# Masked prefix sums of eight sequences, gathered at the midpoint: how the fixed first rows are loaded, and in which order listed rows go to partitions

## The chip, the cores and the metric

One core of one Trainium2 chip runs the kernel. The metric is device time in microseconds (us). Three runs of the kernel before gave 178.06, 178.50 and 179.37 us, a median of 178.5 us.

## What is computed

```
B, S, D = 8, 8192, 512            # x [B, S, D] float32, w [D, D] float32
lengths = randint(16, S, size=(B,))   # int64
mask = pos < lengths[:, None, None]
cs = cumsum(x * mask, axis=1)
mid_features = cs[arange(B), lengths // 2]
out = mid_features @ w            # [B, D]
```

The prefix sum is wanted at one place alone, so the kernel sums, for each of the 8 sequences, the rows 0 to lengths // 2 that lie below its length, and multiplies the 8 sums by w. The lengths of this draw are 1138, 5379, 511, 4113, 1809, 7542, 7716 and 1140; they are data on the chip, so the kernel learns only at run time how many rows it needs.

## The kernel before

Four rows of one sequence are one unit: 8 KB that lie together in memory. The work has three stages.

**Blind rows.** The first 256 rows (64 units) of every sequence are loaded without knowing its length. `sync` (lines 110 to 116) issues four transfers on SP's queue, each for a pair of sequences: 2 x 64 units into the 128 partitions of `xf[:, f]`, 1 MB each. Partitions 0 to 63 hold the even sequence, 64 to 127 the odd one. `s_front[f]` counts the landing.

**Listed rows.** VectorE reads the lengths and makes a list of all other units that are needed: `k_f` units for each sequence, 3161 in all for this draw. The list is cut into 25 chunks of 128, and the first chunk number (c = 0) is filled up with 39 places that fetch nothing. `rank` says which place of a chunk a partition serves: 13 times the partition's number, modulo 128. `idx` is the unit to fetch, for each partition and chunk. `gpsimd` waits for the number of chunks (`count`) and for a zeroed `xz` (`s_zero`, line 171), jumps into the middle of a long sequence of written-out code by a tree of branches (`enter`, lines 130 to 145), and issues from there one indirect transfer per chunk (line 159), from the highest chunk down to 0. Chunks 24 to 1 go into the ring `xt` of R = 8 buffers; each takes one of 8 tokens (`s_free`), which TensorE gives back when it has summed a chunk. Chunk 0 goes to `xz`. Behind the list POOL issues the two transfers of w.

**Sums and product.** TensorE waits for the four blind tiles in order, sums each by 4 matmuls (one for each row u of a unit; they stand in four column groups of the array and run side by side; weights `wf` are 0 or 1 by sequence and length), then jumps into its own sequence of code by the same tree, and sums chunk by chunk with the weights `wc`. All sums gather in `s_ps`, in four partition groups of 8. Behind chunk 0, `pe_tail` closes the four groups with 4 matmuls of 8 columns that add zero (line 312), VectorE copies `s_ps` in four quarters (`s_sb`), 4 matmuls with `fold` transpose them and add the four groups (line 318), and 16 matmuls with w (line 326) give the output, which SP and ACT store.

Of the kernel before, what the change touches and what calls it, by code (L numbers as in the profile page):

```python
# [8 lines left out]
I32 = mybir.dt.int32  # L9
ALU = mybir.AluOpType  # L10
AX = mybir.AxisListType
P = 128
# [3 lines left out]
def kernel(  # L16
# [4 lines left out]
    w: bass.AP,  # L21
    out: bass.AP,
):

# [5 lines left out]
    B, S, D = x.shape  # L32
    U = 4
# [3 lines left out]
    HEAD = 256  # L37
# [9 lines left out]
    def sb(name, shape, dt=F32):  # L47
        return ctx.enter_context(nc.sbuf_tensor(name, shape, dt))
# [4 lines left out]
    def sem(name):  # L53
        return tc.alloc_semaphore(name)

    xf = sb("xf", [P, PAIRS, U * D])
    xt = sb("xt", [P, R, U * D])
    xz = sb("xz", [P, U * D])
    wt = sb("wt", [P, KC, D])
# [8 lines left out]
    row = sb("row", [1, 4 * B])  # L68
    ones = sb("ones", [1, P])
    zero = sb("zero", [1, D])  # L70
    rank_i = sb("rank_i", [P, 1], I32)
    rank_m = sb("rank_m", [P, 1], I32)
    rank4 = sb("rank4", [P, 1])
    rank = sb("rank", [P, 1])
    q_i = sb("q_i", [P, C], I32)
# [8 lines left out]
    early = sb("early", [P, C, U, B])  # L84
    wc = sb("wc", [P, C, U, B])
    wf = sb("wf", [P, PAIRS * (U * B + 2)])
    fold_i = sb("fold_i", [P, B], I32)
    fold_m = sb("fold_m", [P, B], I32)
    fold = sb("fold", [P, B, 4])
# [8 lines left out]

    s_full = [sem(f"full{c}") for c in range(C)]
    s_front = [sem(f"front{k}") for k in range(PAIRS)]  # L100
    s_w = [sem(f"w{k}") for k in range(2)]
    s_len, s_out, s_pool, s_dve, s_pe, s_free, s_zero = (
        sem(n) for n in ("len", "out", "pool", "dve", "pe", "free", "zero"))
# [4 lines left out]


    def sync(sp):  # L110
        for f in range(PAIRS):
            sp.dma_start(out=xf[:, f],
                         in_=x[2 * f:2 * f + 2, :HEAD].rearrange("b (q u) d -> b q (u d)", u=U),
                         ).then_inc(s_front[f], 16)
        store(sp, 0)
        sp.wait_ge(s_out, 32)


    def scalar(act):
        act.dma_start(out=lens[:], in_=lens_words).then_inc(s_len, 16)  # L120
        act.memzero(xz[:]).then_inc(s_zero, 1)  # L121
        store(act, 2)

    def store(eng, j):
# [22 lines left out]


    def gpsimd(pool):
        pool.iota(rank_i[:], pattern=[[0, 1]], base=0, channel_multiplier=13)  # L150
        pool.iota(q_i[:], pattern=[[P, C]], base=0, channel_multiplier=0).then_inc(s_pool, 1)
        pool.iota(f_i[:], pattern=[[1, U]], base=0, channel_multiplier=U)
        pool.iota(fold_i[:], pattern=[[-1, B]], base=128, channel_multiplier=1)
        pool.iota(v_i[:], pattern=[[P * U, C], [1, U]], base=HEAD, channel_multiplier=0,  # L154
                  ).then_inc(s_pool, 1)
        pool.sem_inc(s_free, R)

        def gather(to, c):
            pool.indirect_dma_start(  # L159
                out=to, out_offset=None, in_=xu,  # L160
                in_offset=bass.IndirectOffsetOnAxis(ap=idx[:, c:c + 1], axis=0),
                bounds_check=B * UB - 1, oob_is_err=False,
            ).then_inc(s_full[c], 16)

        n = pool.alloc_register("n_pool")
        pool.wait_ge(s_dve, marks["count"])
        pool.load(n, count[:])
        pool.wait_ge(s_zero, 1)
        enter(pool, "gp", n)
        for c in range(C - 1, -1, -1):  # L170
            with nc.body(f"gp_c{c}", valid_engines=[pool.engine]):
                pool.wait_ge(s_dve, marks["idx"])
                if c:
                    pool.sem_inc(s_free, -1)._wait_ge(s_free, 1)  # L174
                    gather(xt[:, c % R], c)
                    pool.br(f"gp_c{c - 1}")  # L176
                else:
                    gather(xz[:], c)
                    pool.br("gp_tail")
        with nc.body("gp_tail", valid_engines=[pool.engine]):  # L180
            pool.dma_start(out=wt[:, :KC - 1],
                           in_=w[:D - P].rearrange("(p k) d -> p k d", k=KC - 1)).then_inc(s_w[0], 16)
            pool.dma_start(out=wt[:, KC - 1], in_=w[LAST]).then_inc(s_w[1], 16)
            pool.drain()
            pool.br(END)
# [5 lines left out]
    def vector(dve):  # L191
        def step(do, *args, **kw):
            if done[0]:
                dve.wait_ge(s_dve, done[0])
            do(*args, **kw).then_inc(s_dve, 1)  # L195
            done[0] += 1
# [8 lines left out]
        step(dve.memset, zero[:], 0.0)  # L205
        step(dve.memset, ones[:], 1.0)
        mark("ones")
        dve.wait_ge(s_pool, 1)
        step(ts, out=rank_m[:], in0=rank_i[:], scalar1=P - 1, scalar2=None, op0=ALU.bitwise_and)
        step(ts, out=rank[:], in0=rank_m[:], scalar1=0.0, scalar2=None, op0=ALU.add)  # L210
        step(ts, out=q[:], in0=q_i[:], scalar1=rank[:], scalar2=None, op0=ALU.add)
        step(ts, out=z[:, :, B], in0=q[:], scalar1=float(FAR), scalar2=None, op0=ALU.add)
        dve.wait_ge(s_len, 16)
# [27 lines left out]
        step(dve.tensor_reduce, out=idx[:], in_=z[:], axis=AX.X, op=ALU.add)  # L241
        mark("idx")
        step(dve.memset, wf[:], 0.0)
        dve.wait_ge(s_pool, 2)
        step(ts, out=f_m[:], in0=f_i[:], scalar1=HEAD - 1, scalar2=None, op0=ALU.bitwise_and)
        diag = wf[:].rearrange("p (f e) -> p f e", f=PAIRS)
        for h in range(2):
# [2 lines left out]
                 in0=f_m[at].unsqueeze(1).to_broadcast((64, PAIRS, U)),  # L250
                 in1=rows[at, h::2].unsqueeze(2).to_broadcast((64, PAIRS, U)), op=ALU.is_lt)
        mark("front")
        step(ts, out=rank4[:], in0=rank_m[:], scalar1=float(U), scalar2=None, op0=ALU.mult)
        step(ts, out=v4[:], in0=v_i[:], scalar1=rank4[:], scalar2=None, op0=ALU.add)
        step(tt, out=early[:].rearrange("p c u b -> p (c u) b"),
             in0=v4[:].unsqueeze(2).to_broadcast((P, C * U, B)),
# [1 line left out]
        step(tt, out=wc[:], in0=early[:], in1=ge[:].unsqueeze(2).to_broadcast((P, C, U, B)),  # L258
             op=ALU.mult)
        step(ts, out=fold_m[:], in0=fold_i[:], scalar1=31, scalar2=None, op0=ALU.bitwise_and)  # L260
        step(dve.memset, fold[:], 0.0)
        step(ts, out=fold[:, :, 0], in0=fold_m[:], scalar1=0, scalar2=None, op0=ALU.is_equal)
        mark("w")
# [11 lines left out]


    def tensor(pe):
        def add(j, weights, rows):
            return pe.matmul(s_ps[32 * j:32 * j + B], lhsT=weights, rhs=rows,  # L279
                             start=False, stop=False, skip_group_check=True,  # L280
                             tile_position=(0, 32 * j))

        n = pe.alloc_register("n_pe")
        pe.wait_ge(s_dve, marks["ones"])
        for to, width in ((s_ps, D), (o_ps, P)):
            for j in range(4):
                pe.matmul(to[32 * j:32 * j + 32, :width], lhsT=zero[:, :32], rhs=zero[:, :width],  # L287
                          start=True, stop=False, skip_group_check=True, tile_position=(0, 32 * j))
        pe.wait_ge(s_dve, marks["row"])
        pe.matmul(bc_ps[:, :4 * B], lhsT=ones[:], rhs=row[:], start=True, stop=True,  # L290
                  ).then_inc(s_pe, 1)
        pe.load(n, count[:])
        pe.wait_ge(s_dve, marks["front"])
        for f in range(PAIRS):
            pe.wait_ge(s_front[f], 16)
            for u in range(U):
                at = (f * U + u) * B
                add(u, wf[:, at:at + B], xf[:, f, u * D:(u + 1) * D])
        pe.wait_ge(s_dve, marks["w"])
        enter(pe, "pe", n)  # L300
        for c in range(C - 1, -1, -1):
            with nc.body(f"pe_c{c}", valid_engines=[pe.engine]):
                pe.wait_ge(s_full[c], 16)
                rows = xt[:, c % R] if c else xz[:]
                for u in range(U):
                    mm = add(u, wc[:, c, u], rows[:, u * D:(u + 1) * D])
                if c:
                    mm.then_inc(s_free, 1)
                pe.br(f"pe_c{c - 1}" if c else "pe_tail")
        with nc.body("pe_tail", valid_engines=[pe.engine]):  # L310
            for j in range(4):
                mm = pe.matmul(s_ps[32 * j:32 * j + 32, :8], lhsT=zero[:, :32], rhs=zero[:, :8],  # L312
                               start=False, stop=False, skip_group_check=True,
                               tile_position=(0, 32 * j))
            mm.then_inc(s_pe, 1)
            for k in range(KC):
                pe.wait_ge(s_dve, marks["s"] - KC + k + 1)
                pe.matmul(mf_ps[k][:, :4 * B], lhsT=s_sb[:, k * P:(k + 1) * P],  # L318
                          rhs=fold[:].rearrange("p b r -> p (b r)"),
                          start=True, stop=True).then_inc(s_pe, 1)  # L320
            for k in range(KC):
                pe.wait_ge(s_dve, marks["mf"] - KC + k + 1)
                if k in (0, KC - 1):
                    pe.wait_ge(s_w[k // (KC - 1)], 16)
                for j in range(4):
                    mm = pe.matmul(o_ps[32 * j:32 * j + 32, :P], lhsT=mf_sb[:, k],  # L326
                                   rhs=wt[:, k, j * P:(j + 1) * P], start=False,
                                   stop=(k == KC - 1), skip_group_check=True,
                                   tile_position=(0, 32 * j))
            mm.then_inc(s_pe, 1)  # L330
            pe.br(END)
# [41 lines left out]
```

## Time and profile before

| | us |
|---|---|
| median of the three runs | 178.5 |
| the profiled execution | 178.0 |
| its span, first to last instruction | 175.9 |
| PE busy | 48.7 |
| POOL busy | 28.3 |
| DVE busy | 13.7 |

The profiled execution took 178.0 us, of which 175.9 us are the span and 2.1 us lie around it. No compute engine is busy for 30% of the span. The transfers move 31.25 MB: 4.20 MB on SP's queue (the blind rows and half of the output) and 26.95 MB on POOL's (the listed rows, 25.9 MB, and w, 1.05 MB). "DMA share" is the mean busy share of the 16 DMA engines in a stretch, "GB/s" what they moved.

### The profile page before, as it was taken

Reading aid. Unit: us, or ns where it says so; the run is one execution under the profiler, and the core shown is the slowest. Engines: PE = TensorE matmul, PEld = TensorE weight load, DVE = VectorE, ACT = ScalarE, POOL = GpSimd, SP = SyncE. Lnnn points to the kernel's source line nnn. Section 1 sums busy time; section 2 is a strip of 40 time slices with the busy share of each in tenths; the row PEclk is TensorE's granted clock in tenths of the full one; section 3 lists DMA queues with packets and bytes.
Section 4 is the critical chain, followed back from the end, with each engine's and each line's share of the span. In section 5 each row is a group of like instructions: output and inputs, shape, how many; then the busy total and the mean of one; then the engine's idle time right before and its main releaser. Section 6 shows DMA issues by size and latency. Waiting matters only on the chain. (4 is left out here: it accounts for less than half of the span.)

```text
span 175.9 us, 843 instructions
## 1 busy us (share of the span) xinstructions
PE 48.7 (28%) x298; PEld 7.4 (4%) x298; DVE 13.7 (8%) x41; ACT 3.2 (2%) x2; POOL 28.3 (16%) x36
## 2 busy tenths in 40 slices
PE   5100000004000000400040000439728756677590
PEld 1100000000000000000000000002100000000040
DVE  5793000000000000000000000000000000000040
ACT  6000000000000000000000000000000000000000
POOL 3078400000000000000000000005774445200000
PEclk9999999999999999999999999999985585856798
DMA  0159999951111111111111110003999999999800
GB/s 17 56 181 345 335 306 313 311 168 50 56 52 52 54 52 54 52 54 52 54 54 52 54 52 39 4 7 86 360 421 438 421 417 417 429 425 419 366 29 4
DMA packets 4389, 31.25 MB, mean 178 GB/s; under 512 B 485, under 2 KB 517, under 8 KB 709
## 3 DMA queue, kind: packets, MB, share of 16 engines
q0 software_dynamic: 3824, 26.95, 40.6%
q1 hardware_dynamic: 538, 4.20, 5.9%
q8 instruction: 5, 0.08, 0.2%
q14 instruction: 2, 0.02, 0.0%
q10 hardware_dynamic: 20, 0.01, 0.0%
HBM read 31.46 MB, written 0.02 MB: 179 GB/s over the span
## 5 line engine op out<-in xcount | busy, mean ns | idle before, releaser
L159 POOL DMA_INDIRECT xt<-in_x_dram,idx x24 | 24.7, 1031 | 120.9 <-POOLq L174 110.0
L279 PE MATMUL s_ps<-xt,wc 128*8 128x512 f32 x192 | 33.9, 820 | 20.5 <-DMA xt<-in_x_dram,idx 15.3
L279 PE MATMUL s_ps<-xf,wf 128*8 128x512 f32 x32 | 7.6, 1041 | 98.4 <-DMA xf<-in_x_dram 98.4
L195 DVE COPY s_sb<-s_ps 128x128 f32<-128x128 f32 x4 | 1.2, 291 | 154.1 <-PE s_ps L312 154.0
L279 PEld LDWEIGHTS s_ps<-xt,wc 128*8 128x8 f32 x192 | 3.7, 92 | 50.8 <-DMA xt<-in_x_dram,idx 38.0
L279 PEld LDWEIGHTS s_ps<-xf,wf 128*8 128x8 f32 x32 | 0.5, 91 | 103.9 <-DMA xf<-in_x_dram 70.2
L287 PE MATMUL s_ps<-zero 1*32 1x512 f32 x8 | 1.9, 1055 | 1.9 <-DVE ones L195 1.9
L195 DVE TENSOR_TENSOR wc<-early,ge 128x1952 f32<-128x1952 f32 x1 | 2.2, 2243 | 0.0
L195 DVE TENSOR_TENSOR early<-v,bc_ps 128x1952 f32<-128x1952 f32 x1 | 2.2, 2186 | 0.0
L121 ACT ACTIVATE xz<-xz 128x2048 uint32<-128x2048 uint32 x1 | 1.9, 1909 | 0.0
L279 PE MATMUL s_ps<-xz,wc 128*8 128x512 f32 x8 | 1.5, 832 | 0.6 <-DMA xz<-in_x_dram,idx 0.6
L318 PE MATMUL mf_ps<-fold,s_sb 128*128 128x32 f32 x8 | 1.4, 286 | 0.4 <-DVE s_sb L195 0.4
L121 ACT ACT_TABLE_LOAD x1 | 1.3, 1283 | 1.5 <-SPq L45 1.5
L326 PE MATMUL o_ps<-wt,mf_sb 128*32 128x128 f32 x32 | 1.3, 285 | 0.0
L318 PEld LDWEIGHTS mf_ps<-fold,s_sb 128*128 128x128 f32 x8 | 1.2, 188 | 0.6 <-DVE s_sb L195 0.5
L159 POOL DMA_INDIRECT xz<-in_x_dram,idx x1 | 1.0, 987 | 0.3 <-issue 0.3
L290 PE MATMUL bc_ps<-row,ones 1*128 1x32 f32 x2 | 0.6, 406 | 1.0 <-DVE row L195 1.0
L154 POOL IOTA v_i<- 128x244 int32 x1 | 0.8, 819 | 0.0
L195 DVE COPY mf_sb<-mf_ps 128x32 f32<-128x32 f32 x4 | 0.8, 192 | 0.4
L195 DVE TENSOR_REDUCE idx<-z 128x61 int32<-128x549 f32 x1 | 0.7, 726 | 0.0
L195 DVE TENSOR_TENSOR ge<-q,bc_ps 128x488 f32<-128x488 f32 x1 | 0.7, 662 | 0.7 <-PE bc_ps L290 0.7
L195 DVE TENSOR_TENSOR z<-ge,bc_ps 128x488 f32<-128x488 f32 x1 | 0.7, 661 | 0.0
(43 smaller groups left out, 10.3 us busy)
## 6 DMA issues: line engine op xcount, KB each, us to landing
xf<-in_x_dram SPq DMA_DIRECT2D x4, 1024.0 KB
wt<-in_w_dram POOLq DMA_DIRECT2D x1, 768.0 KB, 19.6
xt<-in_x_dram,idx POOLq DMA_INDIRECT x24, 17.5
wt<-in_w_dram POOLq DMA_DIRECT2D x1, 256.0 KB, 19.6
lens<-in_lengths_dram ACTq DMA_DIRECT2D x1, 0.1 KB
xz<-in_x_dram,idx POOLq DMA_INDIRECT x1, 18.7
out_dram<-o_sb SPq DMA_DIRECT2D x1, 8.0 KB
out_dram<-o_sb ACTq DMA_DIRECT2D x1, 8.0 KB
```

The source lines that it names most:

```text
L121: act.memzero(xz[:]).then_inc(s_zero, 1)
L154: pool.iota(v_i[:], pattern=[[P * U, C], [1, U]], base=HEAD, channel_multiplier=0,).then_inc(s_pool, 1)
L159: pool.indirect_dma_start(out=to, out_offset=None, in_=xu, in_offset=bass.IndirectOffsetOnAxis(ap=idx[:, c:c + 1], axis=0), bounds_check=B ...
L195: do(*args, **kw).then_inc(s_dve, 1)
L279: return pe.matmul(s_ps[32 * j:32 * j + B], lhsT=weights, rhs=rows, start=False, stop=False, skip_group_check=True, tile_position=(0, 32 * j))
L287: pe.matmul(to[32 * j:32 * j + 32, :width], lhsT=zero[:, :32], rhs=zero[:, :width], start=True, stop=False, skip_group_check=True, tile_po ...
L290: pe.matmul(bc_ps[:, :4 * B], lhsT=ones[:], rhs=row[:], start=True, stop=True,).then_inc(s_pe, 1)
L318: pe.matmul(mf_ps[k][:, :4 * B], lhsT=s_sb[:, k * P:(k + 1) * P], rhs=fold[:].rearrange("p b r -> p (b r)"), start=True, stop=True).then_i ...
L326: mm = pe.matmul(o_ps[32 * j:32 * j + 32, :P], lhsT=mf_sb[:, k], rhs=wt[:, k, j * P:(j + 1) * P], start=False, stop=(k == KC - 1), skip_gr ...
```

## The change

Three things change. The blind rows come as eight transfers, one per sequence, of 64 units each into 64 partitions; of the last sequence only rows 128 to 255 come this way (32 units), and ACT zeroes the 32 partitions that stay empty. The places of a chunk are dealt to partitions by another formula (four `iota` of 32 partitions and a multiply-add on VectorE in place of the factor 13). The 128 rows left out are fetched last, behind chunk 0 and ahead of w, one row per partition (`xb`), and summed in `pe_tail` by 4 matmuls of 128 columns, one for each quarter of the columns; these take the place of the four closing matmuls.

```diff
     def sync(sp):
-        for f in range(PAIRS):
-            sp.dma_start(out=xf[:, f],
-                         in_=x[2 * f:2 * f + 2, :HEAD].rearrange("b (q u) d -> b q (u d)", u=U),
-                         ).then_inc(s_front[f], 16)
+        for b in range(B):
+            skip = P if b == B - 1 else 0
+            at = 64 * (b % 2)
+            sp.dma_start(out=xf[at + skip // U:at + HU, b // 2],
+                         in_=x[b, skip:HEAD].rearrange("(q u) d -> q (u d)", u=U),
+                         ).then_inc(s_front[b // 2], 16)
...
     def scalar(act):
         act.dma_start(out=lens[:], in_=lens_words).then_inc(s_len, 16)
-        act.memzero(xz[:]).then_inc(s_zero, 1)
+        act.memzero(xz[:])
+        act.memzero(xf[64:64 + P // U, PAIRS - 1]).then_inc(s_zero, 1)
...
     def gpsimd(pool):
-        pool.iota(rank_i[:], pattern=[[0, 1]], base=0, channel_multiplier=13)
+        for k in range(4):
+            pool.iota(base[32 * k:32 * k + 32], pattern=[[0, 1]],
+                      base=64 * (k % 2) + 8 * (k // 2) + 63 * 8 * k,
+                      channel_multiplier=16).then_inc(s_pool, 1)
+        pool.wait_ge(s_pool, 4)
+        pool.iota(p_i[:], pattern=[[0, 1]], base=0, channel_multiplier=1)
         pool.iota(q_i[:], pattern=[[P, C]], base=0, channel_multiplier=0).then_inc(s_pool, 1)
...
         with nc.body("gp_tail", valid_engines=[pool.engine]):
+            pool.dma_start(out=xb[:], in_=x[B - 1, :P]).then_inc(s_back, 16)
             pool.dma_start(out=wt[:, :KC - 1],
...
-        dve.wait_ge(s_pool, 1)
-        step(ts, out=rank_m[:], in0=rank_i[:], scalar1=P - 1, scalar2=None, op0=ALU.bitwise_and)
-        step(ts, out=rank[:], in0=rank_m[:], scalar1=0.0, scalar2=None, op0=ALU.add)
+        dve.wait_ge(s_pool, 5)
+        step(ts, out=p4[:], in0=p_i[:], scalar1=2, scalar2=None, op0=ALU.logical_shift_right)
+        step(stt, out=rank[:], in0=p4[:], scalar=-63.0, in1=base[:], op0=ALU.mult, op1=ALU.add)
...
         step(dve.memset, wf[:], 0.0)
-        dve.wait_ge(s_pool, 2)
+        step(dve.memset, wb[:], 0.0)
+        dve.wait_ge(s_pool, 6)
...
+        step(tt, out=wb[:, B - 1:], in0=p_i[:], in1=rows[:, B - 1:], op=ALU.is_lt)
...
         for f in range(PAIRS):
-            pe.wait_ge(s_front[f], 16)
+            pe.wait_ge(s_front[f], 32)
+            if f == PAIRS - 1:
+                pe.wait_ge(s_zero, 1)
...
         with nc.body("pe_tail", valid_engines=[pe.engine]):
+            pe.wait_ge(s_back, 16)
             for j in range(4):
-                mm = pe.matmul(s_ps[32 * j:32 * j + 32, :8], lhsT=zero[:, :32], rhs=zero[:, :8],
-                               start=False, stop=False, skip_group_check=True,
-                               tile_position=(0, 32 * j))
+                mm = add(j, wb[:], xb[:, j * P:(j + 1) * P], slice(j * P, (j + 1) * P))
             mm.then_inc(s_pe, 1)
```

With the new formula the places e, e + 16, e + 32 and so on of a chunk fall to partitions 4m to 4m + 3 and 32 partitions further, where m = e for e below 8; for e = 8 to 15 they fall to the upper 64 partitions in the same way.

What SP issues at the start, before (`xf` are the blind rows; the sizes are those of the tile that is written):

```order
4 L112 DMA xf<-in_x_dram 128x1x2048 x4
5 L126 DMA out_dram<-o_sb 2x8x128
6 L341 UNCONDITIONAL_BRANCH
7 L45 NO_OP
8 L368 UNCONDITIONAL_BRANCH
```

And now:

```order
4 L120 DMA xf<-in_x_dram 64x2048 x7
5 L120 DMA xf<-in_x_dram 32x2048
6 L135 DMA out_dram<-o_sb 2x8x128
7 L359 UNCONDITIONAL_BRANCH
8 L47 NO_OP
```

Four transfers of 128 partitions became seven of 64 and one of 32. On ACT, before:

```order
2 L120 DMA lens<-in_lengths_dram 1x16
3 L121 ACT_TABLE_LOAD
4 L121 ACTIVATE xz<-xz 128x2048
5 L126 DMA out_dram<-o_sb 2x8x128
6 L341 UNCONDITIONAL_BRANCH
```

And now, with the second zeroing, behind which POOL's and TensorE's waits for `s_zero` now stand:

```order
2 L128 DMA lens<-in_lengths_dram 1x16
3 L129 ACT_TABLE_LOAD
4 L129 ACTIVATE xz<-xz 128x2048
5 L130 ACTIVATE xf<-xf 32x2048
6 L135 DMA out_dram<-o_sb 2x8x128
```

The end of the list on PE, before (`xz` is chunk 0, `s_ps` the sums):

```order
156 L135 COMPARE_AND_BRANCH
157 L279 MATMUL s_ps<-xz,wc 8x512 x4
158 L309 UNCONDITIONAL_BRANCH
159 L312 MATMUL s_ps<-zero 32x8 x4
160 L318 MATMUL mf_ps<-fold,s_sb 128x32 x4
161 L326 MATMUL o_ps<-wt,mf_sb 32x128 x16
```

And now, with the matmuls on the 128 rows that come last:

```order
156 L144 COMPARE_AND_BRANCH
157 L296 MATMUL s_ps<-xz,wc 8x512 x4
158 L328 UNCONDITIONAL_BRANCH
159 L296 MATMUL s_ps<-xb,wb 8x128 x4
160 L336 MATMUL mf_ps<-fold,s_sb 128x32 x4
161 L344 MATMUL o_ps<-wt,mf_sb 32x128 x16
```

The four matmuls of row 159 changed in place; nothing else moved on PE.

## Rows read from the trace of the kernel before

**Rows 1.** The page: 40 equal slices of the span (4.4 us each).
```profile
DMA  0159999951111111111111110003999999999800
GB/s 17 56 181 345 335 306 313 311 168 50 56 52 52 54 52 54 52 54 52 54 54 52 54 52 39 4 7 86 360 421 438 421 417 417 429 425 419 366 29 4
```

**Rows 2.** The longest waits of the whole span: waiting, waited for, total us, times, longest.
```profile
POOL xt L159 <- POOLq L174: 110.0, 10, 99.8
PE s_ps L279 <- DMA xf<-in_x_dram: 98.4, 4, 33.5
PE s_ps L279 <- issue: 5.2, 1, 5.2
```

**Rows 3.** Timeline of the head: SP's four issues and the first alone, ACT, DVE, POOL.
```profile
0.97 65.96 SPq L112 DMA_DIRECT2D xf<-in_x_dram  x4
...
0.97 0.68 SPq L112 DMA_DIRECT2D xf<-in_x_dram  x1
...
2.76 1.91 ACT L121 ACTIVATE xz<-xz 128x2048 uint32<-128x2048 uint32 x1
...
3.72 0.14 DVE L195 TENSOR_SCALAR count<-up_i 1x1 int32<-1x1 int32 x1
...
9.08 1.19 POOL L159 DMA_INDIRECT xt<-in_x_dram,idx  x1 [6.78 <-DVE wf L195]
...
19.16 0.99 POOL L159 DMA_INDIRECT xt<-in_x_dram,idx  x1 [0.30 <-issue]
```

**Rows 4.** Timeline of PE: first and last of four blind tiles, then chunks; start us, us.
```profile
39.46 1.90 PE L279 MATMUL s_ps<-xf,wf 128*8 128x512 f32 x8 [33.55 <-DMA xf<-in_x_dram]
...
110.03 1.90 PE L279 MATMUL s_ps<-xf,wf 128*8 128x512 f32 x8 [17.79 <-DMA xf<-in_x_dram]
...
117.15 9.39 PE L279 MATMUL s_ps<-xt,wc 128*8 128x512 f32 x72 [5.23 <-issue]
```

**Rows 5.** Two longer stages, in the same columns.
```profile
64.00:108.00 44.00, 3.79 (x16) 0.24 (x16) 0.00 (x0) 0.00 (x0) 0.00 (x0) 1.00 0.13 53
128.00:165.00 37.00, 23.13 (x116) 1.80 (x120) 0.00 (x0) 0.00 (x0) 11.90 (x13) 0.67 1.01 422
```

**Rows 6.** Timeline of PE's weight loads, chunk 1 and chunk 0 as they land.
```profile
164.47 0.12 PEld L279 LDWEIGHTS s_ps<-xt,wc 128*8 128x8 f32 x8 [2.38 <-DMA xt<-in_x_dram,idx]
166.96 0.12 PEld L279 LDWEIGHTS s_ps<-xz,wc 128*8 128x8 f32 x8 [2.37 <-DMA xz<-in_x_dram,idx]
```

**Rows 7.** The page's DMA queues, POOL's and SP's: packets, MB, share of 16 engines.
```profile
q0 software_dynamic: 3824, 26.95, 40.6%
q1 hardware_dynamic: 538, 4.20, 5.9%
```

**Rows 8.** Stages: from:to, length, busy us per engine, PEclk, DMA share, GB/s.
```profile
0.00:5.00 5.00, 2.35 (x16) 0.58 (x16) 3.13 (x17) 3.19 (x2) 1.43 (x9) 1.00 0.07 21
...
20.00:25.00 5.00, 0.00 (x0) 0.00 (x0) 0.00 (x0) 0.00 (x0) 0.15 (x1) 1.00 1.04 318
...
30.00:35.00 5.00, 0.00 (x0) 0.00 (x0) 0.00 (x0) 0.00 (x0) 0.00 (x0) 1.00 1.02 313
...
125.00:130.00 5.00, 2.34 (x24) 0.23 (x16) 0.00 (x0) 0.00 (x0) 3.79 (x4) 1.00 0.97 387
```

**Rows 9.** The chain that ended last, in order of time: start us, us, what.
```profile
148.22 18.70 DMA xz<-in_x_dram,idx
...
166.97 1.47 PE s_ps L279 x8
168.44 0.22 PE s_ps L312 x8
...
170.41 1.24 PE o_ps L326 x32
```

**Rows 10.** The later transfer of w: its issue in the timeline, then issue to landing.
```profile
149.77 0.60 POOL L183 DMA_DIRECT2D wt<-in_w_dram  x1
...
wt<-in_w_dram POOLq DMA_DIRECT2D x1, 256.0 KB, 19.6
```

More of the change, by code (lines that the diff above doesn't have):

```diff
@@ L56 @@
     xf = sb("xf", [P, PAIRS, U * D])
+    xb = sb("xb", [P, D])
     xt = sb("xt", [P, R, U * D])
@@ L70 @@
     zero = sb("zero", [1, D])
-    rank_i = sb("rank_i", [P, 1], I32)
-    rank_m = sb("rank_m", [P, 1], I32)
+    p_i = sb("p_i", [P, 1], I32)
+    p4 = sb("p4", [P, 1], I32)
+    base = sb("base", [P, 1], I32)
     rank4 = sb("rank4", [P, 1])
@@ L86 @@
     wf = sb("wf", [P, PAIRS * (U * B + 2)])
+    wb = sb("wb", [P, B])
     fold_i = sb("fold_i", [P, B], I32)
@@ L100 @@
     s_front = [sem(f"front{k}") for k in range(PAIRS)]
+    s_back = sem("back")
     s_w = [sem(f"w{k}") for k in range(2)]
@@ L252, in vector @@
         mark("front")
-        step(ts, out=rank4[:], in0=rank_m[:], scalar1=float(U), scalar2=None, op0=ALU.mult)
+        step(ts, out=rank4[:], in0=rank[:], scalar1=float(U), scalar2=None, op0=ALU.mult)
         step(ts, out=v4[:], in0=v_i[:], scalar1=rank4[:], scalar2=None, op0=ALU.add)
@@ L277, in tensor, with add @@
     def tensor(pe):
-        def add(j, weights, rows):
-            return pe.matmul(s_ps[32 * j:32 * j + B], lhsT=weights, rhs=rows,
+        def add(j, weights, rows, cols=slice(0, D)):
+            return pe.matmul(s_ps[32 * j:32 * j + B, cols], lhsT=weights, rhs=rows,
                              start=False, stop=False, skip_group_check=True,
```

## The prediction, made before the changed kernel ran

> **What bounds the kernel now.** I read the slices of the page first. The DMA engines are full twice, for some 20 us near the start and 40 us before the end; between them lie about 80 us in which they move 50 GB/s and then almost nothing [rows 1]. The list of waits says who stands there: POOL waits 99.8 us at a stretch for a token to issue its next gather, and TensorE waits 98.4 us for the blind rows [rows 2]. These are one wait: POOL has issued 8 gathers by 20.2 us [rows 3], the ring is full, and tokens come back only when TensorE has summed a chunk, which in its program stands behind the four blind tiles. The first of them is summed at 39.5 us, the fourth at 110.0, and the first chunk at 117.2 [rows 4].
>
> So the blind rows bound the first 110 us. When they are alone they move at 53 GB/s with a DMA share of 0.13, which is 2 of 16 engines, 26.5 GB/s each [rows 5]. Two is also the number of sequences in one transfer. With all 16 busy on gathers the rate is 422 GB/s, again 26.4 for each [rows 5], and a chunk of 1.05 MB lands every 2.49 us [rows 6]. After 117 us the kernel is bound by these transfers alone: TensorE's burst took 9.39 us for 9 chunks, 1.04 each at the 2.4 GHz level [rows 4]; even the slowest group of four in these rows, 1.90, is under 2.49.
>
> **The change part by part.** One transfer per sequence hands 64 units, not 2 sequences, as its outermost dimension. I take it that these are dealt over 16 engines, 4 units each. The 4.19 MB of blind rows then need no longer 110 us. TensorE's wait of 98.4 us goes, and with it POOL's. What is late next is the volume itself: 26.95 MB on POOL's queue and 4.20 on SP's [rows 7], over 16 engines. The sum follows the bytes.
>
> *Start.* In the first 5 us of before, 21 GB/s, 0.105 MB, were moved [rows 8]; at 53 GB/s these take 2.0 us, so data flows from 3.0 us. SP was held for 65.96 us by its four issues, of which the first alone took 0.68 [rows 3]; the later ones waited behind two engines with 64 units of each transfer. With 4 units per engine I expect eight issues like the first, 5.5 us, ahead of the data they start.
>
> *Gathers start later.* POOL waits for `s_zero` before it enters its code. Before, the zeroing ended at 2.76 + 1.91 = 4.67, `count` stood at 3.86 and the first gather was issued at 9.08 [rows 3], 4.4 behind the zeroing. Now a second zeroing of the same width, 1.9 us, lies ahead of that signal: 6.6 us, first gather at 11.0, first data some 2 us later, at 13.1 (before, the slices show the engines filling about 2 us behind 9.08 [rows 1]). Behind the waiting POOL stand all gathers. Until then blind rows fill the engines, so the delay is covered unless these are through before 13.1. POOL's four extra iotas and VectorE's three extra instructions (0.14 for the one shown [rows 3]) are below 1 us and lie inside the same cover.
>
> *Rate of the blind rows.* No row shows blind rows on 16 engines. The top is 422 GB/s. The nearest row with blind and gathered rows in flight together is 20 to 35 us: engines full (share 1.00 to 1.04), yet only 313 to 318 GB/s [rows 8]. I take 313. The bottom is half of 422, 211 GB/s, reached if writing into 64 of the 128 partitions gives half of the paths.
>
> The Trainium skill states just that: "SBUF — State Buffer", section "Door 1: The DMA port swizzle (why `[64,N]` ≈ `[32,N]`)", says that partitions 0 to 63 reach only 8 of 16 ports and measured 196 GB/s there against 328 for 128 partitions. By it the sum would stand at the bottom; this case's trace has no transfer of that shape on 16 engines to show it. Its page "DMA: Bandwidth & Descriptors", section "Back-pressure in remote DMA", says that stalled writes hold up an engine's other queues too; the 313 to 318 GB/s at full share [rows 8] fit this, but do not prove it.
>
> *Sum.* Blind rows by SP's queue: 8 x 0.524 - 0.262 = 3.93 MB. From 3.0 to 13.1 at 313 GB/s 3.16 MB are through. The other 0.77 MB share the engines evenly with 0.77 MB of gathers: 1.54 / 0.313 = 4.9 us, to 18.0. TensorE then sums the last blind tile (1.9) and enters its chunk code (5.2 [rows 2]), about 25 us. By then the 8 issued gathers have 8.39 - 0.77 = 7.6 MB left at 18.0, 18 us of work, so tokens come back in time and the engines never run dry; that cover is gone only if the blind rows land after about 30 us. The gathers are POOL's 26.95 MB less 1.05 of w, 25.90. Remaining: 25.90 - 0.77 = 25.13 MB at 422: 59.5, to 77.5. A settling loss as at 125 to 130 us (387 in place of 422 for 5 us [rows 8]): 0.4. Chunk 0 lands at 77.9.
>
> *Even dealing.* Chunk 0 moves 89 units of 128, but landed 2.49 us behind the chunk before it, as a full one does [rows 6]: some engine had 8. By the new formula none has more than 6, some 1.86 us. This 0.6 us is in the sum already, as I counted bytes.
>
> *The end.* Before, chunk 0 landed at 148.22 + 18.70 = 166.92 and the span ended at 175.9: 8.95 us, of which 1.47 + 0.22 are its sums and the closing matmuls [rows 9]. Now 0.26 MB of `xb` land 0.62 behind chunk 0, which its 1.47 us of matmuls hide. The closing becomes 4 matmuls of 128 columns; 16 of those took 1.24 [rows 9], so 4 take 0.31, and waiting and starting them apart I allow 0.25 more than before: 9.2 in all. Bounds: 0 if the overlap is as good as before, 1 if xb lands late. w lies 0.62 later: its later part landed at 149.77 + 19.6 = 169.4 [rows 10], and the matmuls on w run from 170.41 [rows 9]; a slack of 1.0 becomes some 0.6 (0.62 later, used 0.25 later), so nothing. Without that slack each 0.1 us would cost 0.1.
>
> So the span is 77.9 + 9.2 = 87.1, with 2.1 around it 89.2. The median of the runs lies 0.5 above the profiled execution; I forecast 89.7 us.
>
> **The rivals.** *Full rate.* The blind rows run at 422: done at 3.0 + 9.3 = 12.3, before the gathers' data at 13.1. Then 13.1 + 25.90 / 0.422 = 74.5, and with 0.4, 9.2, 2.1 and 0.5 it is 86.7. For it: two engines alone reach their full 26.5 each [rows 5]; against it: the 313 at full share.
>
> *Half rate.* At 211 GB/s 2.13 MB are through at 13.1. For the other 1.80 MB and as much of gathers, three of four packets would go to one half: 2/3 of 422, 281 GB/s, 12.8 us, to 25.9. Then 24.1 / 0.422 = 57.1: 83.0, and 95.2 in all. The port rule quoted above is this rival.
>
> *Slow gathers.* The 313 to 318 GB/s may not be the mixture but the first 8 chunks themselves, the units of the last sequences. Then 8.39 MB take 26.8 in place of 19.9: 6.9 more, on top of the full rate 93.6, on top of the forecast up to 96.6. For it: 14 of the 16 engines had no blind rows then, and yet the whole was a quarter slower. Against it: the later chunks, also consecutive units, ran at 422.
>
> *It doesn't do what it says, and is slower.* If one transfer of one sequence, which is one unbroken piece of memory, went to a single engine, the blind rows would take 3.93 MB / 26.5 GB/s = 148 us, to 151. From the last blind tile on, before needed 178.0 - 110.0 = 68.0 us: 219 us, plus nothing hidden. It decides once the blind rows move below 3.93 MB / 107 us = 37 GB/s. For it: two sequences went with two engines. Against it: the program's rows show 64 x 2048 with 64 outermost.
>
> **How the numbers follow.** Forecast (between 88 and 92): 0.40. Half rate: 0.27. Full rate: 0.17. Slow gathers: 0.11. A gather rate that stays at 313 throughout (25.1 / 0.313 = 80 in place of 59.5, about 110 us): 0.03. One engine: 0.02. The range goes from 85.0, a little under full rate, to 97.5, above half rate and slow gathers. A change of 1% is about what can be told from none here. Faster by over 1%: 0.98; within: 0.00; slower: 0.02.
>
> **What would show it.** Right: SP's eight issues over by 10 us; blind tiles summed before 25 us; POOL's first gather at about 11; no slice of the DMA below 7 tenths between 4 and 78 us; chunks landing every 2.49 us once the blind rows are in; VectorE's copy of `s_ps` about 2 us after chunk 0. Wrong: blind rows at 211 or 422 GB/s in the stage from 5 to 13 us name a rival at once; stages above 25 us at 313 name slow gathers; tokens that POOL waits for while the DMA share falls mean that TensorE's entry has become the bound; a first blind tile after 30 us means few engines.

## The result and the profile after

| | before | after |
|---|---|---|
| median of the runs, us | 178.28 | 95.96 |
| ratio to before, 95% interval | 1 | 0.5377 (0.5349 to 0.5405) |
| profiled execution, us | 178.0 | 95.83 |
| its span, us | 175.9 | 93.7 |
| blind rows on the move, GB/s | 53 | 215 to 226 |
| gathers alone, GB/s | 422 | 421 |

Some executions of these kernels take 0.8 to 3.5 us longer than the rest, most of them at a lower granted clock; the medians leave them out, but the traces of two experiments ("The dealing of before" and "The first part alone") are of such executions. The time fell by 82.3 us, nearly to half. The range given, 85.0 to 97.5 us, holds the time; the forecast itself, 89.7 us, is 6.3 us too low, and the half-rate rival's 95.2 is 0.8 off. What happened is that rival, not the rate that the forecast chose.

The slices of the changed kernel's page answer to [rows 1]; a slice is now 2.3 us:

```profile
DMA  0999999999999999999999999999999999995000
GB/s 0 238 224 224 220 224 213 224 224 399 413 420 430 406 423 413 420 416 430 413 427 416 430 427 413 430 402 427 416 430 416 427 413 430 408 410 227 9 10 4
```

The engines are full from the second slice almost to the end; the long empty stretch is gone. But eight slices, from 2.3 to 21.1 us, move only 213 to 238 GB/s at full share. The engines are busy there and carry half of what they carry later.

The stages of the changed kernel, in the columns of [rows 8]:

```profile
5.00:10.00 5.00, 0.86 (x6) 0.62 (x10) 3.66 (x14) 1.59 (x1) 0.00 (x0) 1.00 1.00 215
10.00:15.00 5.00, 3.55 (x16) 0.12 (x8) 4.86 (x5) 0.00 (x0) 0.00 (x0) 1.00 1.00 215
15.00:20.00 5.00, 1.76 (x10) 0.12 (x8) 0.39 (x3) 0.00 (x0) 3.38 (x4) 1.00 1.05 226
...
25.00:30.00 5.00, 0.00 (x0) 0.00 (x0) 0.00 (x0) 0.00 (x0) 0.99 (x1) 1.00 1.01 415
30.00:35.00 5.00, 0.54 (x4) 0.13 (x8) 0.00 (x0) 0.00 (x0) 0.00 (x0) 1.00 1.01 418
...
26.00:70.00 44.00, 23.11 (x144) 2.94 (x144) 0.00 (x0) 0.00 (x0) 18.54 (x20) 0.87 1.01 421
```

215 GB/s from 5 to 15 us is 0.51 of the 421 that the gathers reach (last row). The two rows from 25 to 35 us are of the same first chunks that ran at 313 to 318 in the kernel before [rows 8]: here they run at full rate, with no blind rows in flight.

The timeline of the changed kernel: SP's issues, ACT's zeroings, POOL's first gather, the last blind tile and the first chunks. It answers to [rows 3, 4].

```profile
0.97 5.04 SPq L120 DMA_DIRECT2D xf<-in_x_dram  x8
...
2.76 1.91 ACT L129 ACTIVATE xz<-xz 128x2048 uint32<-128x2048 uint32 x1
...
4.68 1.91 ACT L130 ACTIVATE xf<-xf 32x2048 uint32<-32x2048 uint32 x1
...
15.71 1.19 POOL L173 DMA_INDIRECT xt<-in_x_dram,idx  x1 [12.62 <-POOLq L188]
...
22.04 1.90 PE L296 MATMUL s_ps<-xf,wf 128*8 128x512 f32 x8 [1.90 <-DMA xf<-in_x_dram]
...
34.46 8.04 PE L296 MATMUL s_ps<-xt,wc 128*8 128x512 f32 x56 [10.52 <-issue]
```

SP is free after 6.0 us, the last blind tile is summed at 22.0 in place of 110.0. Two things are later than foreseen: the first gather, issued 9.1 us behind the second zeroing's end at 6.59, and TensorE's entry into its chunk code, 10.5 us in place of 5.2. A third thing is seen only in the packet records of the trace: the first gather, issued at 15.7, moves its first packet at 20.0 us, and the last packet of the blind rows ends at 21.0. Blind rows and gathers hardly ran beside each other.

The chain that ended last, answering to [rows 9]:

```profile
64.71 17.86 DMA xt<-in_x_dram,idx
82.57 0.04 issue
82.61 3.93 PE s_ps L296 x24
86.54 0.02 issue
86.56 0.30 DVE s_sb L210
```

The last transfer in the chain is chunk 1, not chunk 0: from 82.61 on TensorE works without a pause on chunk 1, chunk 0 and xb (8 records each).

### The profile page after: what moved, and what is told of

The parts are those of the page before. It is cut to its first block, busy times and chain, and to the rows that moved or that the text cites. A ratio compares the mean times of both kernels' runs of the same rounds, so it can differ in the third digit from the quotient of the medians.

```text
span 93.7 us, 856 instructions
## 1 busy us (share of the span) xinstructions
PE 48.6 (52%) x298; PEld 7.4 (8%) x298; DVE 14.2 (15%) x43; ACT 5.1 (5%) x3; POOL 28.7 (31%) x41
## 5 line engine op out<-in xcount | busy, mean ns | idle before, releaser
L173 POOL DMA_INDIRECT xt<-in_x_dram,idx x24 | 24.0, 1001 | 38.6 <-POOLq L188 34.4
L130 ACT ACTIVATE xf<-xf 32x2048 uint32<-32x2048 uint32 x1 | 1.9, 1905 | 0.0
L160 POOL IOTA base<- 32x1 int32 x4 | 0.5, 124 | 0.8 <-SPq L47 0.6
## 6 DMA issues: line engine op xcount, KB each, us to landing
xz<-in_x_dram,idx POOLq DMA_INDIRECT x1, 18.4
```

What stands on the lines that cost most here:

```text
L130: act.memzero(xf[64:64 + P // U, PAIRS - 1]).then_inc(s_zero, 1)
L160: pool.iota(base[32 * k:32 * k + 32], pattern=[[0, 1]], base=64 * (k % 2) + 8 * (k // 2) + 63 * 8 * k, channel_multiplier=16).then_inc(s_p ...
L173: pool.indirect_dma_start(out=to, out_offset=None, in_=xu, in_offset=bass.IndirectOffsetOnAxis(ap=idx[:, c:c + 1], axis=0), bounds_check=B ...
```

## The experiments

Two theories stood against each other after the result. *Halves*: a transfer into 64 partitions of one half reaches half of the ways into the chip's memory, so blind rows run at half rate. *Queue*: SP's queue, or transfers of 0.5 MB, give 215 GB/s wherever they write. The code fences are excerpts: `...` and the remarks behind `#` are added, and lines that only follow from an edit are left out.

**Blind rows over all partitions.** Two rows a partition in place of four; zeroing, weights and matmuls follow.

```diff
-            at = 64 * (b % 2)
-            sp.dma_start(out=xf[at + skip // U:at + HU, b // 2],
-                         in_=x[b, skip:HEAD].rearrange("(q u) d -> q (u d)", u=U),
+            sp.dma_start(out=xf[skip // V:, b],          # V = 2
+                         in_=x[b, skip:HEAD].rearrange("(q v) d -> q (v d)", v=V),
...
```

> The changed kernel, but every sequence's 64 blind units are laid out as 128 half units of 2 rows over all 128 partitions (the last sequence's 128 rows over the upper 64). Halves theory (a transfer into 64 partitions of one half reaches half of the paths, so the blind rows ran at 215 GB/s): the blind rows move at about 415 GB/s from 3 us on and are in by 13 us; the first gather, issued at 15.7 in the changed kernel, limits what is left, so 90 to 93.5 us. Queue theory (SP's queue, or transfers of 0.5 MB, give 215 GB/s wherever they write): blind rows at 215 GB/s until 20 us, 96 us as before.

Measured: 89.91 us, ratio 0.5068 (0.5044 to 0.5093), 6.0 us faster than the changed kernel and just below the expected span. Its stages, in the same columns:

```profile
5.00:10.00 5.00, 1.28 (x6) 0.62 (x10) 3.70 (x13) 0.64 (x1) 0.00 (x0) 1.00 1.02 411
10.00:15.00 5.00, 4.53 (x32) 0.69 (x24) 4.79 (x6) 0.00 (x0) 3.10 (x2) 1.00 0.78 247
15.00:20.00 5.00, 0.10 (x4) 0.00 (x0) 0.18 (x1) 0.00 (x0) 3.78 (x5) 0.92 0.97 377
```

From the same queue, with the same 0.5 MB each, the blind rows move at 411 GB/s. The queue theory falls. From 10 to 15 us the engines are no longer full: now the gathers' start is bare.

**An earlier start of the gathers.** The zeroing signal is split, so that POOL waits for the first zeroing alone.

```diff
-        act.memzero(xz[:])
+        act.memzero(xz[:]).then_inc(s_zero, 1)
         act.memzero(xf[64:64 + P // U, PAIRS - 1]).then_inc(s_zero, 1)
...
-                pe.wait_ge(s_zero, 1)
+                pe.wait_ge(s_zero, 2)
```

> The changed kernel with the zeroing signal split, so that POOL waits for the first zeroing alone and TensorE for both. The first gather moves from 15.7 to between 10 and 14 us, so that gathers run beside blind rows. Halves theory: blind rows alone use half of the paths, mixed with gathers two thirds (281 GB/s), so some 6 us of mixing gain 0.9 us: 95.1 us, at most 1.5 faster. Queue theory: the gathers find the other half of every engine free and mix at 420 GB/s: 3 us faster, 93 us. If the gathers' start does not matter at all: 96.0.

Measured: 95.05 us, ratio 0.5365 (0.5335 to 0.5394): 0.9 us faster, though the two intervals overlap. That is the size that halves give, but not for their reason. A stage of this kernel, in the same columns, and two pieces of the chain that ended last:

```profile
15.00:20.00 5.00, 2.12 (x12) 0.12 (x8) 0.65 (x3) 0.00 (x0) 3.80 (x4) 1.00 1.03 224
...
65.69 18.44 DMA xz<-in_x_dram,idx
...
84.17 1.31 PE s_ps L296 x16
```

The first gather is issued at 14.14 in place of 15.71 (so the delay is not the zeroing alone), yet the rate stays at half, 224 GB/s and not 281 or 420. In the packet records the first gather's data move from 19.9 us, where they moved from 20.0 in the changed kernel. The mixing for which both theories gave a price did not take place, and this run does not decide between them. Of the 1.0 us by which the profiled execution is shorter, 0.3 lie ahead of chunk 0's landing (84.13 against 84.4 us). The sums of chunk 0 and xb make up most of the rest: 1.31 us at a granted clock of 1.00, where the changed kernel, at 0.50 from 84 to 86 us, needed 2.0.

**Both edits.** The two diffs above together.

> Both edits: blind rows over 128 partitions and the split zeroing signal. Halves theory: blind rows in by 12.5, first gather issued at about 11, data from 13, engines full almost throughout: 87 to 90 us. Queue theory: as with the split signal alone, 93 us.

Measured: 89.60 us, ratio 0.5038 (0.5004 to 0.5072). Within what halves gave; the split signal adds 0.3, which the intervals do not tell from nothing. The first gather is issued at 10.94 in place of 11.60.

**The disputed cost by itself.** A program of loads alone, stage by stage, executed once. Of its lines the fence shows the transfers; loops and waits are left out.

```diff
+            sp.dma_start(out=xf[:64, b], in_=rows(b, 0, 256))        # 0 to 63, 8 times
+            sp.dma_start(out=xf[32:96, b], in_=rows(b, 256, 256))    # 32 to 95, 8 times
+            sp.dma_start(out=xf[:, b, :2 * D], in_=rows(b, 512, 256, 2))
+            sp.dma_start(out=xf[:64, b], in_=rows(b, 768, 256))      # even b, and beside it
+            act.dma_start(out=xf[64:, b], in_=rows(b, 768, 256))     # odd b
+            pool.dma_start(out=xt[:, k], in_=rows(6, 512 * k, 512))  # alone, 8 times
+            act.dma_start(out=xf[:, 0], in_=pair(0, 1024, 256))      # beside 8 more of pool's
+            act.dma_start(out=xf[:8, k], in_=pair(0, 1280 + 16 * k, 16))  # the same
```

> Leaves out the whole computation: it only moves rows of x into the chip, in stages one behind the other, and stores zeros. Stages, with the halves theory's rates: 8 transfers of 64 units into partitions 0 to 63: 215 GB/s; the same into partitions 32 to 95: about 415; the same rows as half units into all 128: about 415; even sequences into 0 to 63 on SP's queue beside odd ones into 64 to 127 on ACT's: 215 to 415; 8 plain loads of 128 units on POOL's queue alone: 420; the same beside one transfer of 2 x 64 units on two engines: 300 to 320, as at 20 to 35 us of the kernel before; the same beside two-engine transfers that write only the 4 partitions which these engines serve anyway: about 420. Queue theory: 215 in each stage on SP's queue. If memory, not the way into the chip, made the mixture slow, the last stage is at 300 to 320 too.

A stretch inside each stage, in their order (from:to, length, DVE, POOL, PEclk, DMA share, GB/s):

```profile
5.00:22.00 17.00, 0.00 (x0) 0.00 (x0) 1.00 1.01 206
32.00:36.00 4.00, 0.00 (x0) 0.00 (x0) 1.00 0.99 418
46.00:49.00 3.00, 0.00 (x0) 0.00 (x0) 1.00 1.00 408
54.00:68.00 14.00, 0.00 (x0) 0.00 (x0) 1.00 1.01 232
78.00:92.00 14.00, 0.00 (x0) 0.00 (x0) 1.00 1.01 425
102.00:118.00 16.00, 0.00 (x0) 0.00 (x0) 1.00 1.02 308
...
150.00:162.00 12.00, 0.00 (x0) 0.00 (x0) 1.00 1.01 427
```

Row 1 against row 2: same queue, sizes and number of partitions; 0 to 63 gives 206 GB/s, 32 to 95 gives 418 once settled (311 from 26 to 30 us, in the first transfers). So what counts is that both halves are written, not how many partitions. Row 3 is the end of its stage; from 38 to 44 us the same transfers ran at 317 to 358, for which no run here has a cause. Row 6 rebuilds the mixture of the kernel before: loads of 128 partitions that run at 425 alone fall to 308, all queues together, when a transfer of two engines (53 GB/s alone, from 128 to 140 us) writes across all partitions. In row 7 two engines again carry another queue's transfers, but write only partitions 0 to 7: 427. The rows are read in much the same way, so the writing is the likely cause of the slow mixture. The two stages differ in one thing more, transfers of 64 KB in place of one of 1 MB, and no row shows which engine writes which partitions.

**The dealing of before.**

```diff
-        for k in range(4):
-            pool.iota(base[32 * k:32 * k + 32], pattern=[[0, 1]],
...
+        pool.iota(rank_i[:], pattern=[[0, 1]], base=0, channel_multiplier=13)
...
```

> The changed kernel with the dealing of before (places 13 times the partition, modulo 128). The prediction's even dealing was worth 0.6 us: chunk 0's slowest engine has 8 units in place of 6. So chunk 0 comes 2.5 us behind chunk 1, not 1.9: 96.6 us. Rival: chunk 1's matmuls at the low clock, 1.9 us, already cover what the dealing saves, or other engines lag by more: 96.0, no difference.

Measured: 95.97 us, ratio 0.5367 (0.5318 to 0.5416). No difference can be told, but the interval reaches 0.9 us to either side, so the 0.6 is not excluded either. The weight loads of chunk 1 and chunk 0 in the timeline of this kernel:

```profile
82.61 0.12 PEld L292 LDWEIGHTS s_ps<-xt,wc 128*8 128x8 f32 x8 [2.37 <-DMA xt<-in_x_dram,idx]
84.99 0.12 PEld L292 LDWEIGHTS s_ps<-xz,wc 128*8 128x8 f32 x8 [2.26 <-DMA xz<-in_x_dram,idx]
```

And the same two of the changed kernel:

```profile
82.61 0.12 PEld L296 LDWEIGHTS s_ps<-xt,wc 128*8 128x8 f32 x8 [2.37 <-DMA xt<-in_x_dram,idx]
84.50 0.12 PEld L296 LDWEIGHTS s_ps<-xz,wc 128*8 128x8 f32 x8 [1.76 <-DMA xz<-in_x_dram,idx]
```

Even dealing does bring chunk 0 earlier, 1.89 in place of 2.38 us behind chunk 1. In the changed kernel it could not be summed sooner than that: TensorE takes 1.90 for chunk 1 in this stretch (granted clock 0.65 from 82 to 84 us, 0.50 from 84 to 86, the 1.2 GHz level), and chunk 0 lands at 84.4, just before it is free. So some 0.5 us are gained up to the start of chunk 0; whether they reach the total is not shown.

**Without the third part.** All 256 rows of the last sequence come blind, the closing matmuls of before are back.

```diff
-            skip = P if b == B - 1 else 0
+            skip = 0
...
-            pool.dma_start(out=xb[:], in_=x[B - 1, :P]).then_inc(s_back, 16)
...
-                mm = add(j, wb[:], xb[:, j * P:(j + 1) * P], slice(j * P, (j + 1) * P))
+                mm = pe.matmul(s_ps[32 * j:32 * j + 32, :8], lhsT=zero[:, :32], rhs=zero[:, :8],
...
```

> The changed kernel without its third part: all 256 rows of the last sequence come blind, the closing matmuls of before are back, and no second zeroing is needed. Halves theory: 0.26 MB more at 215 GB/s before the list, 1.2 us; POOL starts 1.9 us earlier, worth 0.6 as with the split signal; the end without xb 0.2 us shorter: 96.3 to 96.5. Rival: xb covers the sums of chunk 0, as it seems meant to, and its loss costs over 1 us more: 97.5.

Measured: 96.14 us, ratio 0.5399 (0.5359 to 0.5439). Against the changed kernel no difference can be told; against the one with the split signal, whose POOL starts about as early (14.14 against 14.50 us here), xb seems to be worth 1.1 us, about the 1.2 of its bytes at half rate, though these intervals overlap too. In the traces chunk 0 lands at 85.86 us here and at 84.13 there.

**The first part alone.** Both of the last two edits: the kernel before with eight transfers.

> The kernel before with the first part of the change alone: eight transfers of one sequence each. If the first part carries the whole gain, 96.5 to 97.2 us (the two other parts are worth 0.3 to 1.2 together). If the three parts work only together, over 99.

Measured: 97.61 us, ratio 0.5461 (0.5425 to 0.5498), 0.4 above the expected span. So the first part brings 80.7 of the 82.3 us, the other two together some 1.7. Without xb the dealing seems to be worth 1.5 (97.61 against 96.14, though the intervals of their ratios still overlap a little). The weight loads of chunk 0 come 1.88 us behind those of chunk 1 with it and 2.49 without it, which would explain 0.6 of that.

**A faster version: 384 blind rows over all partitions.** The gap of 10 to 20 us is to be filled with rows that would otherwise be listed.

```diff
-    HEAD = 256
+    HEAD = 384                                          # V = 3; skip = 0, no xb
...
```

> An attempt at a faster kernel: 384 blind rows of each sequence, 3 to a partition over all 128 partitions, no xb, no second zeroing. Blind rows: 6.29 MB, in by about 18 us, so that the engines stay full until the gathers have started (with 256 rows spread they moved only 292 and 370 GB/s between 10 and 20 us, about 2.4 us lost). 23 chunks in place of 25; some 0.5 MB are read in vain. Halves theory with that gap filled: 87.5 to 88.7 us, against 89.6 with 256 rows. If the wider blind stage only delays POOL's code by as much: 89.6 to 90.5.

Measured: 90.89 us, ratio 0.5096 (0.5045 to 0.5147), a miss. The gap is filled (419 GB/s from 10 to 15 us), but a new one opens where none was expected (two stages of this kernel, same columns):

```profile
25.00:35.00 10.00, 0.96 (x4) 0.00 (x0) 0.00 (x0) 0.00 (x0) 0.00 (x0) 0.67 1.01 419
37.00:41.00 4.00, 4.00 (x24) 0.70 (x20) 0.00 (x0) 0.00 (x0) 1.98 (x2) 0.60 0.55 180
```

The 8 gathers issued early are through at 37 us, and POOL got its next token only at 37.9.

**The same with 11 buffers.**

```diff
-    R = 8
+    R = 11
```

> The kernel with 384 blind rows and a ring of 11 buffers in place of 8. With 8, the engines ran dry between 37 and 41 us (98 to 348 GB/s), since TensorE's entry into its chunk code ended only at 35.1 us and tokens came late. If that is the loss, 3 buffers more (7.5 us of transfers) cover it: no stage below 0.95 from 5 to 75 us, 2.5 us faster, 88.0 to 88.7 us. If the dip only moves (TensorE enters its code later still while the engines are full), 90.5 to 91.2.

Measured: 87.71 us, ratio 0.4944 (0.4907 to 0.4981), 0.3 below the expected span, 8 us under the changed kernel and the fastest seen. The same stretch, in the same columns:

```profile
37.00:41.00 4.00, 4.00 (x28) 0.74 (x24) 0.00 (x0) 0.00 (x0) 1.98 (x2) 0.59 1.02 420
```

## Why the prediction was right, and where it was off

- *That the blind rows bound the first 110 us, and the volume what follows*: right. SP's issues ended at 6.0, the last blind tile came before 25 us, no slice fell below 9 tenths until the list was in, chunks landed every 2.49 us. The first part alone shows it: 97.61 us.
- *16 engines for 64 units*: right. The share is 1.00 where 2 sequences outermost gave 0.13. The rival of one engine, 219 us, falls.
- *Rate of the blind rows*: this step failed. "I take 313", from the stage of before in which blind and gathered rows were mixed; it was 215, and the prediction's own sign for this rival, about 211 GB/s in the stage from 5 to 13 us, came true. The row of 313 was not a measurement of 16 engines on blind rows but of gathers beside a transfer of two engines, and the probe gives both: 308 for the mixture, 206 for 64 partitions of one half. The bottom of the bound, half of 422, was the value to take. By that rule, in the Trainium skill's "SBUF — State Buffer", section "Door 1: The DMA port swizzle (why `[64,N]` ≈ `[32,N]`)", the rate follows from the ports that the partitions reach; the trace agrees, 206 GB/s for partitions 0 to 63 and 418 for 32 to 95.
- *Half rate, as rival*: right in the rate and within 0.8 us. It let gathers run beside the blind rows at 281 GB/s from 13.1 us and these end at 25.9. That mixing did not happen: the first gather was issued at 15.7 and moved data from 20.0, the rate stays at half up to 21.1 us and is 399 GB/s in the next slice. For the sum it makes no difference: with the gathers only behind the blind rows, 3.0 + 3.93 / 0.211 + 25.90 / 0.422 is 83.0 as well. So the rival's time holds, and its rate for the mixture, two thirds, stays untested.
- *Slow gathers*: fell. The same eight chunks run at 415 to 418 GB/s when no blind rows are in flight.
- *Gathers start at 11.0*: wrong, 15.7. The prediction took 4.4 us from the zeroing to the first gather, as before; it was 9.1. As foreseen, blind rows covered it: with the split signal the first gather is issued 1.6 us earlier and its data move 0.1 earlier. (VectorE has two instructions more, 43 against 41, not three; nothing hangs on it.)
- *TensorE enters its code in 5.2*: wrong, 10.5. The cover held with 8 buffers in the changed kernel; with wider blind rows it did not, and cost 3.2 us (90.89 against 87.71).
- *Even dealing, 0.6*: right for chunk 0 (1.89 us behind chunk 1, 2.38 without it); its effect on the total is too small for these runs.
- *The end, 9.2 us behind chunk 0*: right. Chunk 0 landed at 84.4 (issued at 66.0, 18.4 us to landing) and the span ended at 93.7, 9.3 us.

The size that was missed is in the main one term, the rate of the blind rows. With 215 GB/s, and the gathers behind them, the prediction's sum ends the list at 3.0 + 18.3 + 61.4 = 82.7 us in place of 77.5: 5.2 of the 6.3. Chunk 0 then landed 1.3 us later than this gives (84.4 against 83.1 with the settling loss), which no run here puts down to a term; the median lies 0.1 above the profiled execution in place of 0.5, which gives 0.4 back.

## What to carry to other kernels

Here a transfer's outermost dimension went with the number of DMA engines that it got (2 sequences: a share of 0.13; 64 units: 1.00), and the partitions that it wrote with what these could do (0 to 63: 206 GB/s; 32 to 95: 418). Look for a stretch with full DMA share and half of the usual GB/s, and spread each transfer over both halves, 0 to 63 and 64 to 127. A rate read from a mixture of transfers is no bound for one of them alone. When a wait of 100 us goes, ask anew what stood hidden in it: here the entry of two engines into their code, and with it the number of buffers.

## What had not been expected

- Even sequences on SP's queue beside odd ones on ACT's, so that both halves have work at every moment, move 232 GB/s (row 4 of the probe), hardly more than 206. The packet records of the trace show why: the engines take the two queues in step. Of the 16 packets in flight, none is SP's at 58.0 us, 16 are at 58.6, none at 59.1 and 16 at 59.6; from 54 to 68 us all packets in flight belong to one queue, and so go into one half, for about half of the time, and nearly all do for two thirds.
- Entering written-out code took longer while the DMA engines were full. TensorE needed 5.2 us from its last blind tile to its first chunk in the kernel before, with idle engines, 10.5 in the changed one and 8.7 to 12.8 in the faster ones; POOL 4.4 and 9.1 us from the zeroing. With the blind rows spread, and so sooner out of the way, POOL needed 6.0 (zeroing over at 5.6, gather at 11.60). The code comes by transfers of its own; the page of the changed kernel lists them:

```profile
q8 instruction: 5, 0.08, 0.4%
q14 instruction: 2, 0.02, 0.1%
```

  In the packet records two packets of q8, 16 KB each, lie about TensorE's entry, starting 3.4 us apart before (111.2 and 114.6 us) and 5.9 apart in the changed kernel (25.9 and 31.8). The first chunk's matmuls begin 1.6 and 1.7 us behind the end of the second packet. POOL's first gather follows a packet of q14 in the same way, by 2.6 and 1.9 us. By these records it is the code that came late. That its transfers wait behind data is likely, but not shown.
- Where a transfer of two engines wrote across all partitions beside loads of 128, the total fell: 308 in place of 425 GB/s at a share of 1.02. The section "Back-pressure in remote DMA" of the Trainium skill's "DMA: Bandwidth & Descriptors" says, of transfers between cores, that a saturated destination port holds up the engines that share the way to it. Row 6 of the probe shows such a loss for loads from the chip's own memory; that a full port is its cause is not shown.
